# q and k of a dilated attention by seven products of quarters

## The chip, the cores and the metric

The kernel runs on one core of a Trainium2 chip. The metric is the device time of one execution in microseconds (us).

## What is computed

Two layers on a sequence of 512 tokens with 1024 features, all float32. Layer 0 has a gated recurrence (HGRN2), layer 1 a dilated attention; each is followed by a SwiGLU feed-forward part. The input of every part is normalised and modulated by vectors made from a condition `c`:

```python
mod = (cond @ ada_w[layer] + ada_b[layer])[:, None, :]
sh1, sc1, g1, sh2, sc2, g2 = jnp.split(mod, 6, axis=-1)
u = rms_norm(h, norm_g[layer, 0]) * (1.0 + sc1) + sh1
y = hgrn2_mixer(...) if layer % 2 == 0 else dilated_attention_mixer(u, cos, sin, w_in, w_out)
h = h + (1.0 + g1) * rms_norm(y, norm_g[layer, 1])
```

The attention has three groups (dilations 1, 4, 16), and in each group q, k and v for 8 heads of 128 features:

```python
proj = (u @ w_in).astype(jnp.float32).reshape(B, S, N_GROUPS, 3, ATT_HEADS, ATT_HEAD_DIM)
for gi, (window, dilation) in enumerate(DILATED_GROUPS):
    q = apply_partial_rope(proj[:, :, gi, 0], cos, sin) * scale     # turns the first 32 features
    k = apply_partial_rope(proj[:, :, gi, 1], cos, sin)
    o_g, lse_g = dilated_group_attention(q, k, proj[:, :, gi, 2], window, dilation)
```

The three groups' outputs are mixed by a softmax over their `lse`.

## The kernel before

Every float32 product is made of three reduced-precision ones (`three`): both operands are split into `hi` (a cast to fp32r, on ScalarE) and `lo` (what is left, on VectorE), and the products hi hi, hi lo and lo hi are added up in one PSUM bank.

Weights come through one queue. `Stream` holds a list of items in the order of their use, loads them by SyncE (SP) into tiles named `raw` (two places of 1 MB; a new tile gets the place that comes free first), and hands out `hi` and `lo` tiles (three places of each). An item is a weight matrix ("w"), a chunk of `ada_w` for the modulation vectors ("ada": four VectorE steps over one raw tile, and after every second chunk an all-reduce over the partitions on GpSimd, POOL in the profile), a pair of rows, a small piece of work ("do"), or "quarters": a weight pair that is cut in four. `weave` sets the ada chunks between the weights: `weave(ws, others, first, every)` puts one group behind each `every`-th weight, from `first` on.

Attention first makes v of the first four heads for three groups (six items, one of them in the stage before), then loops over heads and groups. A turn of this loop takes one weight item with q's and k's columns, makes two `block`s of 24 matmuls of 512 columns into two PSUM banks, evacuates them (`qk_evac`) and turns the first 32 features of both (`turn_pair`, 64 partitions). In between, `fl.tick()` issues work of earlier heads: `scores` (products of q and k, mask, maximum, exponential, and sums that go through DRAM by GpSimd's DMAs, `scr`, `oR`, `oN`), the merge of the groups, transposes (`flip`), products with v. After head 4 stand the v of the last four heads.

The order on each engine in this loop is set by a scheduler at build time; the engines' queues run in order.

The feed-forward parts compute gate and up with seven products instead of eight (`seven_products`): the four quarters of the weights and of the tokens (by feature half and token half) are summed in seven pairs, each product is 128x512 by 512x256, and the results are sums of the seven. The token sums are made once (`token_sums`), the weights' sums for each block: one on GpSimd, two on VectorE (`sum_a`, `sum_b`, `sum_c`), and sums and three of the quarters are split in `hi` and `lo`. Line 791 casts the sums, 795 takes their rest; 767 and 771 do that for the three quarters.

## Time and profile before

| | |
|---|---|
| median of 3 runs | 1515.43 us (1515.34 to 1515.98) |
| profiled execution | 1515.4 us, of which 1513.7 are the span of the trace |
| TensorE busy | 1497.8 us |
| VectorE busy | 1032.8 us |
| ScalarE busy | 692.5 us |
| GpSimd busy | 245.0 us |
| TensorE clock granted | 0.997 |

Busy times are sums over the instructions of an engine; matmuls overlap, so that a busy TensorE isn't one at its peak. Line numbers in the profile are those of the code above. In its rows PE is TensorE's matmuls, PEld its weight loads, DVE VectorE, ACT ScalarE, POOL GpSimd and SP SyncE.

### The profile page before, as it was taken

The page shows a single profiled execution, that of the slowest core. Times are in us where ns is not written, and L with a number is a line of the kernel's source. Part 1 is how long each engine was busy: PE and PEld are TensorE (multiplying, and loading weights), DVE is VectorE, ACT ScalarE, POOL GpSimd, SP SyncE. Part 2 cuts the span into 40 slices and gives each one's busy share as a digit, 9 for nine tenths or more (in the row PEclk, how much of TensorE's full clock was granted, in tenths as well). Part 3 has the DMA queues.
Part 4 walks back from the last instruction along what each step waited for, and adds up shares of the span by engine and source line. Part 5 has one row for each costly group of instructions (what it writes and reads, how often), then busy time and mean ns, then how long its engine had stood idle before and what let it go on. Part 6 is the DMA issues. An engine that isn't in the chain of part 4 may idle for free.

```text
span 1513.7 us, 23113 instructions
## 1 busy us (share of the span) xinstructions
PE 1497.8 (99%) x9111; PEld 1324.4 (87%) x9111; DVE 1032.8 (68%) x1764; ACT 692.5 (46%) x1107; POOL 245.0 (16%) x212
## 2 busy tenths in 40 slices
PE   8999999999999999999999999999999999999998
PEld 6777888899999988889888888988888999999886
DVE  4587867588888896562567686345656978888633
ACT  4443443364444432372456665245645635544231
POOL 1011210051222211140010111000002212221100
PEclk9999999999999999999999999999999999999999
DMA  9654444324333356414644433533212333334521
GB/s 308 185 164 142 153 138 167 112 70 126 112 112 112 116 198 224 138 57 137 167 126 126 125 109 102 153 98 91 78 30 83 100 97 111 107 107 153 205 99 56
DMA packets 207645, 192.83 MB, mean 127 GB/s; under 512 B 6776, under 2 KB 166704, under 8 KB 207536
## 3 DMA queue, kind: packets, MB, share of 16 engines
q1 hardware_dynamic: 206000, 190.87, 41.0%
q8 instruction: 71, 1.16, 0.3%
q0 software_dynamic: 1024, 0.13, 0.2%
q10 hardware_dynamic: 512, 0.35, 0.1%
q14 instruction: 38, 0.31, 0.1%
HBM read 189.17 MB, written 2.16 MB: 126 GB/s over the span
## 4 chain that ended last, share of the span: by engine, by line
PE 93%; issue 2%; ACT 1%; DVE 1%; POOL 1%; DMA 1%; POOLq 0%; DVEq 0%; ACTq 0%
PE ps_mm L417 20%; PE ps_mm L419 20%; PE ps_mm L418 20%; PE ps_b L417 3%; PE ps_b L419 3%; PE ps_b L418 3%; PE ps_a L417 3%; PE ps_a L419 3%; PE ps_a L418 3%; PE ps_mm L1165 1%; PE ps_a L1165 1%; PE ps_a L1610 1%; PE ps_a L1592 1%; PE ps_mm L223 1%; PE ps_a L1659 1%
## 5 line engine op out<-in xcount | busy, mean ns | idle before, releaser
L417 PE MATMUL ps_mm<-uh,hi 128*128 128x512 f32 (+1 forms) x784 | 289.9, 370 | 0.0
L419 PE MATMUL ps_mm<-uh,lo 128*128 128x512 f32 (+1 forms) x784 | 288.6, 368 | 0.0
L418 PE MATMUL ps_mm<-ul,hi 128*128 128x512 f32 (+1 forms) x784 | 287.4, 367 | 0.0
L85 DVE TENSOR_TENSOR lo<-raw,hi 128x2048 fp32r<-128x2048 f32 x74 | 174.7, 2361 | 161.2 <-ACT hi L84 161.0
L84 ACT CAST hi<-raw 128x2048 fp32r<-128x2048 f32 x74 | 141.3, 1909 | 152.4 <-DMA raw<-in_ffn_w_out_dram 49.2
L417 PEld LDWEIGHTS ps_mm<-uh,hi 128*128 128x128 f32 x784 | 147.4, 188 | 31.6 <-issue 8.4
L419 PEld LDWEIGHTS ps_mm<-uh,lo 128*128 128x128 f32 x784 | 147.6, 188 | 23.4
L418 PEld LDWEIGHTS ps_mm<-ul,hi 128*128 128x128 f32 x784 | 147.5, 188 | 22.6
L791 ACT CAST hiq<-raw 128x1024 fp32r<-128x1024 f32 x72 | 72.4, 1052 | 72.4 <-DVE raw L779 71.0
L417 PE MATMUL ps_mm<-hi,oh 128*128 128x512 f32 x240 | 94.1, 392 | 0.0
L418 PE MATMUL ps_mm<-lo,oh 128*128 128x512 f32 x240 | 93.5, 390 | 0.0
L245 DVE SCALAR_TENSOR_TENSOR shared<-raw,cond,shared 128x512 f32<-128x512 f32 x98 | 73.4, 749 | 24.2 <-DMA raw<-in_ada_w_dram 22.5
L795 DVE TENSOR_TENSOR loq<-raw,hiq 128x1024 fp32r<-128x1024 f32 x72 | 84.9, 1219 | 0.0
L247 POOL PARTITION_ALL_REDUCE shared<-shared x12 | 39.9, 3323 | 239.8 <-DVE shared L245 239.8
L419 PE MATMUL ps_mm<-hi,ul 128*128 128x512 f32 x192 | 75.9, 395 | 0.0
L418 PE MATMUL ps_mm<-lo,uh 128*128 128x512 f32 x192 | 75.9, 395 | 0.0
L775 POOL TENSOR_TENSOR raw<-raw 128x512 f32<-128x512 f32 x36 | 57.9, 1608 | 105.4 <-DVE loq L771 45.7
L417 PE MATMUL ps_mm<-hi,uh 128*128 128x512 f32 x192 | 74.5, 396 | 0.0
L779 DVE TENSOR_TENSOR raw<-raw 128x1024 f32<-128x1024 f32 x36 | 44.1, 1225 | 40.9 <-POOL raw L775 40.9
L419 PE MATMUL ps_mm<-hi,ol 128*128 128x512 f32 x176 | 68.5, 389 | 0.0
L825 POOL TENSOR_TENSOR shared<-shared 128x256 f32<-128x256 f32 x36 | 30.2, 840 | 205.8 <-DVE shared L824 205.8
L417 PE MATMUL ps_a<-hi,oh 128*128 128x512 f32 x152 | 59.6, 392 | 0.0
(403 smaller groups left out, 3937.6 us busy)
## 6 DMA issues: line engine op xcount, KB each, us to landing
raw<-in_ada_w_dram SPq DMA_DIRECT2D x40, 1024.0 KB, 5.1
raw<-in_ffn_w_in_dram SPq DMA_DIRECT2D x144, 256.0 KB, 4.1
raw<-in_attn_w_in_dram SPq DMA_DIRECT2D x48, 512.0 KB, 5.1
raw<-in_ffn_w_out_dram SPq DMA_DIRECT2D x22, 1024.0 KB, 4.9
raw<-in_hgrn_w_in_dram SPq DMA_DIRECT2D x12, 1024.0 KB, 5.3
raw<-in_attn_w_in_dram SPq DMA_DIRECT2D x12, 1024.0 KB, 5.1
raw<-in_ffn_w_in_dram SPq DMA_DIRECT2D x8, 1024.0 KB, 5.1
first<-in_ada_w_dram SPq DMA_DIRECT2D x14, 512.0 KB, 7.6
```

Of the source, the lines that this page charges most:

```text
L84: self.nc.scalar.copy(hi, t)
L85: self.nc.vector.tensor_sub(lo, t, hi.bitcast(F32))
L245: dve.scalar_tensor_tensor(a, r[:, k], sc, a, op0=OP.mult, op1=OP.add)
L247: pool.partition_all_reduce(a, a, P, bass.bass_isa.ReduceOp.add)
L417: pe.matmul(ps, ah, bh, start=start, stop=False)
L418: pe.matmul(ps, ah, bl, start=False, stop=False)
L419: pe.matmul(ps, al, bh, start=False, stop=stop)
L775: pool.tensor_add(r[:, 2], r[:, 2], r[:, 0])
L779: dve.tensor_tensor(r[:, 0:2], r[:, 0:3:2], r[:, 1:2].broadcast_to((P, 2, 512)), op=OP.add)
L791: act.copy(hi, src)
L795: dve.tensor_sub(lo, src, hi.bitcast(F32))
L1165: pe.matmul(vbanks[hf, t], a, w, start=e == 0 and which == 0, stop=e == KT - 1 and which == 2)
```

## The change

The loop's two blocks become seven products of quarters as in the feed-forward part, 84 matmuls of 256 columns, into four PSUM banks. A weight item is of kind "quarters" (`aqk`), four loads of 256 KB. `Weights` splits three quarters (lines 1595, 1596), makes three sums on GpSimd (1600, 1604, 1608; 128x512, 128x1024, 128x512) and splits these (1615, 1616); the next pair's weights are prepared while a pair is computed. k and q are put together from the banks by VectorE and ScalarE, and a sum over both halves of k by GpSimd (1664).

The token sums need two tiles of 2 MB. One takes the place of the residual `h` (class `Held`): `h` is stored to DRAM (`kept`, four GpSimd DMAs at the end of the stage before) and loaded again after the loop. The turn now uses 128 partitions with 256 columns (four 32-row copies each way on ScalarE, shuffle and three steps on VectorE); the tables of cosines and sines are laid out for that. The scale of the scores moves into the step with the mask (q and k change sign with it, so the masks do too). `scores` come one tick later. The ada chunks stand behind every item from the third on, not behind every second from the seventh, and their order is (1,4), (1,3), (1,2) instead of (1,2), (1,4), (1,3).

```diff
+ADA_AT = (2, 1)
...
         def aqk(g, hd):
-            return ("w", tuple(AW[:, (g * 3 + k) * D + hd * P:(g * 3 + k) * D + (hd + 1) * P].rearrange(
+            return ("quarters", tuple(AW[:, (g * 3 + k) * D + hd * P:(g * 3 + k) * D + (hd + 1) * P].rearrange(
                 "(k p) n -> p k n", p=P) for k in range(2)))
...
-        items += weave(at, ada_seq((1, 2), (1, 4), (1, 3)), 6, 2)
+        items += weave(at, ada_seq((1, 4), (1, 3), (1, 2)), ADA_AT[0], ADA_AT[1])
...
+                    for t in range(NT):
+                        pool.dma_start(kept[t * P:(t + 1) * P, :], h[:, t])
...
+            def __init__(self):
+                self.raw = st.quarters()
+                self.R = st.part_tiles()
+                act.copy(self.R[0][:, 0:1536], self.raw[:, 512:])
+                dve.tensor_sub(self.R[1][:, 0:1536], self.raw[:, 512:], self.R[0][:, 0:1536].bitcast(F32))
+
+            def sum_a(self):
+                r = Q4(self.raw)
+                pool.tensor_add(r[:, 2], r[:, 2], r[:, 0])
+
+            def sum_b(self):
+                r = Q4(self.raw)
+                pool.tensor_tensor(r[:, 0:2], r[:, 0:3:2], r[:, 1:2].broadcast_to((P, 2, 512)), op=OP.add)
+
+            def sum_c(self):
+                r = Q4(self.raw)
+                pool.tensor_add(r[:, 3], r[:, 3], r[:, 1])
+
+            def parts(self, k):
+                if k == 0:
+                    self.S = st.part_tiles()
+                src = Q4(self.raw)[:, 1:3] if k == 0 else Q4(self.raw)[:, 0:4:3]
+                hi, lo = (Q4(t)[:, 2 * k:2 * k + 2] for t in self.S)
+                act.copy(hi, src)
+                dve.tensor_sub(lo, src, hi.bitcast(F32))
+                if k == 1:
+                    st.fill()
...
+        def qk_pair(hd, g, w, following, ticks):
...
+            run(half(0, 1), w.R, 0, u_of(0, 0))
+            run(half(0, 0), w.R, 512, t_of(2))
+            nxt = following()
+            act.copy(at(slice(1, 3), 0), both(b[0]))
+            run(half(1, 0), w.R, 1024, u_of(1, 0))
+            if nxt:
+                nxt.sum_a()
+                nxt.sum_b()
+            run(half(1, 1), w.S, 0, t_of(3))
+            dve.tensor_tensor(at(slice(0, 3, 2), 0), wide(at(2, 0)), both(b[1]), op=OP.add)
+            if nxt:
+                nxt.parts(0)
+                nxt.sum_c()
+            ticks()
+            run(half(2, 1), w.S, 1024, t_of(1))
+            run(half(2, 0), w.S, 512, t_of(0))
+            dve.tensor_tensor(at(slice(0, 3, 2), 1), wide(at(2, 0)), both(b[2]), op=OP.add)
+            act.copy(at(1, 1), of(half(2, 0)))
+            if nxt:
+                nxt.parts(1)
+            run(half(3, 0), w.S, 1536, u_of(1, 1))
+            dve.tensor_tensor(at(0, 1), at(0, 1), of(half(3, 0)), op=OP.add)
+            pool.tensor_tensor(at(1, every), at(1, every), wide(at(2, 1)), op=OP.add)
+            turn = t[:, 2 * S:2 * S + 256]
+            rot = t[:, 2 * S + 256:3 * S]
...
+            for j in range(4):
+                act.copy(as_of(turn[32 * j:32 * j + 32]), at(j // 2, j % 2)[0:32])
+            dve.stream_shuffle(rot, turn, [(i + 16) % 32 for i in range(32)])
+            dve.tensor_mul(rot, rot, angle[:, 1])
+            dve.tensor_mul(turn, turn, angle[:, 0])
+            dve.tensor_add(turn, turn, rot)
+            for j in range(4):
+                act.copy(at(j // 2, j % 2)[0:32], as_of(turn[32 * j:32 * j + 32]))
+            heads[hd]["k", g], heads[hd]["q", g] = t[:, 0:S], t[:, S:2 * S]
...
+        smx.close()
+        h.again()
+        for t in range(NT):
+            pool.dma_start(h[:, t], kept[t * P:(t + 1) * P, :])
```

What this makes of the queues shows at three places. SP's loads at the start of the loop, before (the number behind `raw` counts the items; 126 and 130 are ada chunks, 127, 128 and from 131 on the pairs):

```order
L66 DMA raw125_8557<-in_attn_w_in_dram 128x4x512
L66 DMA raw126_8563<-in_ada_w_dram 128x4x512
L64 DMA raw127_8673<-in_attn_w_in_dram 128x8x128 x2
L64 DMA raw128_8680<-in_attn_w_in_dram 128x8x128 x2
L66 DMA raw130_8687<-in_ada_w_dram 128x4x512
L64 DMA raw131_8797<-in_attn_w_in_dram 128x8x128 x2
L64 DMA raw132_8814<-in_attn_w_in_dram 128x8x128 x2
```

And now, from the first pair (96) on:

```order
L69 DMA raw95_6622<-in_ada_w_dram 128x4x512
L60 DMA raw96_6628<-in_attn_w_in_dram 128x4x128 x4
L69 DMA raw97_6648<-in_ada_w_dram 128x4x512
L60 DMA raw98_6767<-in_attn_w_in_dram 128x4x128 x4
L69 DMA raw100_6805<-in_ada_w_dram 128x4x512
L60 DMA raw101_6872<-in_attn_w_in_dram 128x4x128 x4
L69 DMA raw102_6947<-in_ada_w_dram 128x4x512
L60 DMA raw103_7014<-in_attn_w_in_dram 128x4x128 x4
```

A pair has four loads for two, and through its first eight pairs each is followed by a chunk of 1 MB.

GpSimd's queue early in the loop, before (ISA without operands is a change of its code library, ISA on `shared` an all-reduce, the DMAs those of the softmax sums):

```order
L247 ISA
L247 ISA shared_90<-shared_90 128x512
L1604 DMA scr_3051<-sN669_6802 128x4x2
L1616 DMA oR691_6991<-scr_3051 128x8
L247 ISA shared_90<-shared_90 128x512
L1622 DMA scr_3051<-sR681_6893 128x8
L1624 DMA oN692_7000<-scr_3051 128x4x2
```

Now, around the weights of the fourth and fifth pair (103 and 106):

```order
L1712 DMA scr_3052<-sN682_7046 128x4x2
L1600 TENSOR_TENSOR raw103_7014<-raw103_7014 128x512
L1724 DMA oR706_7358<-scr_3052 128x8
L1664 TENSOR_TENSOR qk690_7068<-qk690_7068 128x2x4x64
L1604 TENSOR_TENSOR raw103_7014<-raw103_7014 128x1024
L266 ISA
L266 ISA shared_90<-shared_90 128x512
L1608 ISA
L1608 TENSOR_TENSOR raw103_7014<-raw103_7014 128x512
L1600 TENSOR_TENSOR raw106_7164<-raw106_7164 128x512
L1604 TENSOR_TENSOR raw106_7164<-raw106_7164 128x1024
L1608 TENSOR_TENSOR raw106_7164<-raw106_7164 128x512
```

Where the queue held DMAs and all-reduces alone, every weight set now has three sums there and every pair one more; the library changes before an all-reduce and back after it.

VectorE's queue at the same place, now: the last two steps of chunk 105, the turn of the third pair (`qk690`), and behind it the rest of the fourth pair's sums (`loq11`):

```order
L264 SCALAR_TENSOR_TENSOR shared_90<-raw105_7097,cond_89,shared_90 128x512 x2
L1671 STREAM_SHUFFLE qk690_7068<-qk690_7068 128x256
L1672 TENSOR_TENSOR qk690_7068<-qk690_7068,shared_90 128x256
L1673 TENSOR_TENSOR qk690_7068<-qk690_7068,shared_90 128x256
L1674 TENSOR_TENSOR qk690_7068<-qk690_7068 128x256
L1616 TENSOR_TENSOR loq11_7132<-raw103_7014,hiq11_7131 128x1024
```

Before, the loop's weights and its turns stood like this there:

```order
L85 TENSOR_TENSOR lo133_9025<-raw133_8821,hi133_9024 128x2048
L1565 STREAM_SHUFFLE rot935_9017<-turning926_8958 64x512
L1566 TENSOR_TENSOR rot935_9017<-rot935_9017,shared_90 64x512
L1567 TENSOR_TENSOR turning926_8958<-turning926_8958,shared_90 64x512
L1568 TENSOR_TENSOR turning926_8958<-turning926_8958,rot935_9017 64x512
L85 TENSOR_TENSOR lo134_9109<-raw134_8929,hi134_9108 128x2048
```

One rest of 2048 columns a pair became one of 1536 and two of 1024, and the turn's steps are half as long.

More of the change, by code (lines that the diff above doesn't have):

```diff
@@ L109, in quarters @@
     def quarters(self):
+        while self.items[self.done][0] in ("ada", "rows", "do"):
+            self.process_to(self.done + 1)
         assert self.items[self.done][0] == "quarters"
@@ L198, in block_kernel @@
         shared = base.tile([P, 4, S], F32, name="shared")
-        cs = shared[:, 0:2]
+        cs, csr = (shared[:, k].rearrange("p (a n) -> p a n", a=2) for k in range(2))
         cols = base.tile([P, 8, 8], F32, name="cols")
@@ L1335, in tok_proj @@
                     w = slice((kt % 4) * 512, (kt % 4 + 1) * 512)
-                    three(ps, view(uh[:, kt])[t], view(ul[:, kt])[t], whi[:, w], wlo[:, w], kt == 0, kt == KT - 1)
+                    three(ps, *(view(x[kt // 4][:, kt % 4])[t] for x in fu), whi[:, w], wlo[:, w], kt == 0, kt == KT - 1)
                 act.copy(dst[:, t, c0:c0 + 512], ps)
@@ L1562, in turn_pair @@
-        def turn_pair(g, pair):
-            both = pair[0]
-            rot = fresh(mk, [64, S], "rot", 1)
-            dve.stream_shuffle(rot, both, [(i + 16) % 32 for i in range(32)])
-            dve.tensor_mul(rot, rot, cs[0:64, 1])
-            dve.tensor_mul(both, both, cs[0:64, 0])
-            dve.tensor_add(both, both, rot)
-            for k in range(2):
-                dst, src = pair[1 + k][0:32], both[k * 32:k * 32 + 32]
-                act.copy(*((dst, src) if g == 0 else (V4(dst), L4(src))))
+        smx = cx.enter_context(ExitStack())
@@ new lines, in block_kernel @@
+        sums_t = smx.enter_context(tc.tile_pool(name="a_sums", bufs=1)).tile(
+            [P, TPAD + 4096], F32R, name="sums_a")[:, TPAD:]
+        K4 = lambda t: t.rearrange("p (k n) -> p k n", k=4)
+        th_t = fresh(base, [P, NT, D], "h", 1, F32R)
+        th = [K4(th_t[:, k]) for k in range(4)]
+        tl = [K4(sums_t[:, k * 1024:(k + 1) * 1024]) for k in range(4)]
+        u_of = lambda r, c: [tuple(x[r][:, k, c * 256:c * 256 + 256] for x in fu) for k in range(4)]
+        t_of = lambda i: [(th[i][:, k], tl[i][:, k]) for k in range(4)]
@@ new lines, in qk_pair, with run @@
+        def qk_pair(hd, g, w, following, ticks):
+            b = [bank("mm") for _ in range(4)]
+            half = lambda n, k: b[n][:, k * 256:k * 256 + 256]
+            def run(ps, wt, o, us):
+                for kt in range(4):
+                    a = slice(o + kt * P, o + (kt + 1) * P)
+                    three(ps, wt[0][:, a], wt[1][:, a], *us[kt], kt == 0, kt == 3)
+            t = fresh(mk, [P, 3 * S], "qk", 2)
+            if g == 0:
+                at = lambda b_, h_: t.rearrange("p (b h n) -> p b h n", b=3, h=2)[:, b_, h_]
+                of = lambda a: a
+                both = lambda a: H2(a)
+            else:
+                at = lambda b_, h_: t.rearrange("p (b r h l) -> p b h r l", b=3, r=4, h=2)[:, b_, h_]
+                of = lambda a: a.rearrange("p (l r) -> p r l", r=4)
+                both = lambda a: a.rearrange("p (h l r) -> p h r l", h=2, r=4)
+            every = slice(0, 2)
+            wide = lambda a: a.unsqueeze(1).broadcast_to((P, 2) + tuple(a.shape[1:]))
+            run(half(0, 1), w.R, 0, u_of(0, 0))
[23 more added lines that the diff above has]
+            rot = t[:, 2 * S + 256:3 * S]
+            as_of = (lambda a: a) if g == 0 else (lambda a: a.rearrange("p (r l) -> p r l", r=4))
+            angle = cs if g == 0 else csr
+            for j in range(4):
[4 more added lines that the diff above has]
+            dve.tensor_add(turn, turn, rot)
+            for j in range(4):
+                act.copy(at(j // 2, j % 2)[0:32], as_of(turn[32 * j:32 * j + 32]))
+            heads[hd]["k", g], heads[hd]["q", g] = t[:, 0:S], t[:, S:2 * S]
+            ticks()
+            return nxt
@@ L1699, in block_kernel, with following @@
         fl.n = 0
-        for kind, g, i in order[1:]:
+        first_t, last_t = fresh(mk, [P, 3 * S], "qk", 2), fresh(mk, [P, 3 * S], "qk", 2)
+        for j in range(2):
+            token_sums(*([x[:, 2 * j:2 * j + 2] for x in y] for y in (th, tl)),
+                       [H2(first_t[:, k * S:k * S + S]) for k in range(3)] + [H2(last_t[:, j * S:j * S + S])],
+                       slice(2 * j, 2 * j + 2))
+        steps = order[1:]
+        ahead = []
+        def following():
+            w = Weights()
+            ahead.append(w)
+            return w
+        for n_, (kind, g, i) in enumerate(steps):
+            nxt = steps[n_ + 1][0] if n_ + 1 < len(steps) else None
             if kind == "v":
                 tok_proj(V[g], 0, nat if g == 0 else res, (0, 1, 2) if i and g == 0 else ())
+                if nxt == "qk":
+                    w = following()
+                    w.sum_a()
+                    w.sum_b()
+                    w.parts(0)
+                    w.sum_c()
+                    w.parts(1)
                 continue
@@ L1714, in block_kernel @@
                 fl.add(n + 11, lambda i=i: pv_n(i))
-            whi, wlo = st.take()
-            pair = []
-            for k in range(2):
-                ps = block(whi, wlo, k * D, P)
-                heads[i]["qk"[k], g] = qk_evac(ps, g, k, pair)
-                if k == 1:
-                    turn_pair(g, pair)
-                fl.tick()
+            qk_pair(i, g, ahead.pop(0), following if nxt == "qk" else lambda: None, fl.tick)
+        smx.close()
+        h.again()
+        for t in range(NT):
+            pool.dma_start(h[:, t], kept[t * P:(t + 1) * P, :])
         fl.at.clear()
```

64 lines of the change are left out of this document (36 added, 28 removed).

## The prediction

> **What bounds the kernel now.** I read the page first, then the stretches of attention, then single engines there. TensorE works nearly all the time, and the chain that ends last runs through it:
>
> ```profile
> PE 1497.8 (99%) x9111; PEld 1324.4 (87%) x9111; DVE 1032.8 (68%) x1764; ACT 692.5 (46%) x1107; POOL 245.0 (16%) x212
> ...
> PE 93%; issue 2%; ACT 1%; DVE 1%; POOL 1%; DMA 1%; POOLq 0%; DVEq 0%; ACTq 0%
> ```
>
> The stretch table has attention's v part (672 to 728), its whole q/k loop (728 to 1112) and a piece of the loop without modulation work (1040 to 1100):
>
> ```profile
> 672.00:728.00 56.00, 56.00 (x241) 54.08 (x241) 19.22 (x16) 17.03 (x16) 2.14 (x3) 1.00 0.43 125
> 728.00:1112.00 384.00, 384.00 (x1906) 333.30 (x1905) 235.06 (x624) 202.99 (x341) 39.81 (x36) 1.00 0.41 117
> 1040.00:1100.00 60.00, 60.00 (x303) 51.07 (x302) 39.41 (x125) 34.38 (x62) 3.95 (x6) 1.00 0.25 72
> ```
>
> TensorE is full in all three, at clock 1.00; VectorE has 66% in the last, GpSimd almost nothing. So less TensorE work is worth its time, until another engine is slower than what is left. That is the question here, since the change buys TensorE time with VectorE, ScalarE and above all GpSimd time.
>
> The loop's pace, from two matmuls 48 apart, the 48 evacuations of q and k, and the 12 of the three v blocks that interrupt the loop:
>
> ```profile
> 734.67 0.39 PE L418 MATMUL ps_mm<-ul,hi 128*128 128x512 f32 x1
> 745.55 0.39 PE L418 MATMUL ps_mm<-ul,hi 128*128 128x512 f32 x1
> L1557 ACT ACTIVATE qk<-ps_mm x48: 580/594/601, 728.6 to 1107.5; 128x512 f32<-128x512 f32 x48
> L1337 ACT COPY V<-ps_mm x12: 567/587/591, 928.8 to 990.2; 128x512 f32<-128x512 f32 x12
> ```
>
> A pair (q and k of one head in one group) has 48 matmuls: 745.55 - 734.67 = 10.88 us. Eleven steps of v take 61.4, so twelve 67.0. From 728.6 to 1107.5 are 47 half pairs and the v part: (378.9 - 67.0) / 23.5 = 13.27, say 13.2 us for a pair with its share of scores, transposes and weighted sums; those take TensorE 13.2 - 10.88 = 2.3.
>
> **The products.** The new pair has 84 matmuls of 256 columns. The feed-forward part runs the same seven products now; two successive blocks there, by the same step on VectorE:
>
> ```profile
> 454.80 2.35 DVE L795 TENSOR_TENSOR loq<-raw,hiq 128x1024 fp32r<-128x1024 f32 x2
> 464.46 2.36 DVE L795 TENSOR_TENSOR loq<-raw,hiq 128x1024 fp32r<-128x1024 f32 x2
> ```
>
> 9.66 us a block. TensorE's own gain is 10.88 - 9.66 = 1.22 a pair, 29.3 for 24 pairs, and its floor for a pair is 9.66 + 2.3 = 11.95.
>
> **What the helpers pay for a pair.** Groups of the page and of the instruction view (mean ns last but one):
>
> ```profile
> L85 DVE TENSOR_TENSOR lo<-raw,hi 128x2048 fp32r<-128x2048 f32 x74 | 174.7, 2361 | 161.2 <-ACT hi L84 161.0
> L771 DVE TENSOR_TENSOR loq<-raw,hiq 128x1536 fp32r<-128x1536 f32 x18 | 31.6, 1753 | 0.3 <-ACT hiq L767 0.2
> L795 DVE TENSOR_TENSOR loq<-raw,hiq 128x1024 fp32r<-128x1024 f32 x72 | 84.9, 1219 | 0.0
> L1565 DVE STREAM_SHUFFLE rot<-turning 64x512 f32<-64x512 f32 x24 | 17.4, 724 | 0.0
> L1566 DVE TENSOR_TENSOR rot<-rot,shared 64x512 f32<-64x512 f32 x24 | 16.3, 680 | 0.2
> L820 DVE TENSOR_TENSOR shared<-shared,ps_mm 128x512 f32<-128x512 f32 x18 | 12.3, 681 | 4.9 <-PE ps_mm L419 4.9
> L84 ACT CAST hi<-raw 128x2048 fp32r<-128x2048 f32 x74 | 141.3, 1909 | 152.4 <-DMA raw<-in_ffn_w_out_dram 49.2 <-PE ps_mm L418 42.3 <-DMA raw<-in_hgrn_w_in_dram 27.4
> L767 ACT CAST hiq<-raw 128x1536 fp32r<-128x1536 f32 x18 | 26.7, 1482 | 0.0
> L791 ACT CAST hiq<-raw 128x1024 fp32r<-128x1024 f32 x72 | 72.4, 1052 | 72.4 <-DVE raw L779 71.0 <-DVE raw L783 1.3
> L854 ACT COPY shared<-ps_a 128x256 f32<-128x256 f32 x18 | 6.7, 374 | 29.7 <-DVE mid L835 28.1 <-PE ps_b L419 1.6
> ```
>
> VectorE loses the rest of the weights (2.36), the shuffle (0.72) and three turning steps (3 x 0.68): 5.1. It gets the rest of three quarters (1.75), of four sums (2 x 1.22), two sums out of PSUM (2 x 0.68), one of half that (0.35), and the turn on 128 partitions with half the columns (0.36 + 3 x 0.36): 7.4. Net +2.3, on 39.41 / 60 x 13.2 = 8.7 before: 11.0. ScalarE swaps a 1.91 cast for 1.48 + 2 x 1.05, and its copies change little (eight of 32x256, each at most the 0.37 of 128x256): +2 on 34.38 / 60 x 13.2 = 7.6, so under 10: it stays behind TensorE and costs nothing. GpSimd gets everything new: three weight sums and k's sum. Its prices:
>
> ```profile
> L518 POOL TENSOR_TENSOR ul<-u,uh x20: 1277/1301/2538, 306.2 to 1180.4; 128x512 fp32r<-128x512 f32 x20
> L1384 POOL TENSOR_TENSOR k<-T,fsuf x8: 1048/1248/3198, 92.8 to 231.7; 128x512 f32<-128x512 f32 x8
> L247 POOL PARTITION_ALL_REDUCE shared<-shared x12 | 39.9, 3323 | 239.8 <-DVE shared L245 239.8
> 332.77 7.00 POOL L253 PARTITION_ALL_REDUCE shared<-shared  x2 [5.77 <-issue]
> 1.47 0.29 POOL masks.py:199 TENSOR_SCALAR_AFFINE_SELECT ident<-ident 128x128 f32<-128x128 f32 x1 [0.30 <-POOL expo L190]
> POOL oR L1616 <- DMA scr<-sN: 24.9, 8, 3.4
> ```
>
> Undisturbed, a 128x512 sum takes 1.28, so 128x1024 2.56, and one with a broadcast operand 1.05: 1.28 + 2.56 + 1.28 + 1.05 = 6.2 a pair.
>
> **The port.** Three rows of another stage decide the sum. A GpSimd sum and VectorE's L85 start together, then a small VectorE product follows:
>
> ```profile
> 167.97 3.20 POOL L1384 TENSOR_TENSOR k<-T,fsuf 128x512 f32<-128x512 f32 x1 [20.94 <-DVE T L1362]
> 167.97 2.29 DVE L85 TENSOR_TENSOR lo<-raw,hi 128x2048 fp32r<-128x2048 f32 x1
> 170.18 1.27 DVE L1385 TENSOR_TENSOR m<-T,f 128x256 f32<-128x256 f32 x1
> ```
>
> 3.20 is L85's time and then the sum's own 1.05; the 256-column product, worth 0.36, lasts until the GpSimd sum is over. They run one after the other, never together. So I add them. Of VectorE's pair the steps with both inputs in SBUF count: 1.75 + 2.44 + 3 x 0.36 = 5.3. With GpSimd's 6.2 that is 11.5, and about 0.4 of small steps of the softmax weights: 11.9, as much as TensorE's 11.95.
>
> The Trainium skill ("SBUF — State Buffer", section "Who interferes with whom") states this as a rule: a VectorE instruction with two SBUF inputs contends with a GpSimd instruction that reads SBUF, and the later one is blocked to the end. By that rule the addition holds for every pair; if the two shared bandwidth instead, the loop would go by TensorE's floor and VectorE's own 11.0 and 14.5, the first rival below. The three rows above agree with the page.
>
> **The eight pairs with modulation work.** Twelve chunks move from every second to every item, from the second v half on; four fall to the v part, eight to the first eight pairs. A chunk on VectorE, its columns, and the loads:
>
> ```profile
> 707.11 0.49 DVE L243 TENSOR_SCALAR shared<-raw,cond 128x512 f32<-128x512 f32 x1 [1.88 <-DMA raw<-in_ada_w_dram]
> 707.64 2.33 DVE L245 SCALAR_TENSOR_TENSOR shared<-raw,cond,shared 128x512 f32<-128x512 f32 x3
> L262 DVE CUSTOM_DVE_ANT_0 diag<-shared,ident 128x128 f32<-128x128 f32 x32 | 9.1, 286 | 4.1 <-POOL shared L247 3.8
> raw<-in_ada_w_dram SPq DMA_DIRECT2D x40, 1024.0 KB, 5.1
> raw<-in_ffn_w_in_dram SPq DMA_DIRECT2D x144, 256.0 KB, 4.1
> L57 SPq DMA_DIRECT2D raw<-in_ffn_w_in_dram x144: 367/501/788, 347.4 to 1360.2; - x144
> 333.33 3.27 DVE L106 TENSOR_TENSOR lo<-raw,hi 128x1024 fp32r<-128x1024 f32 x1
> ```
>
> VectorE: 11.0 + 2.9 + 4 x 0.29 / 2 = 14.5 a pair. An all-reduce holds the port too: the last row is one that ran beside the first all-reduce (from 332.77). Port: 11.5 + 2.3 + 0.6 + half an all-reduce 1.65 = 16.0. GpSimd by itself for two pairs: 12.4, one all-reduce 3.3, the 5.8 with which it waited for nothing visible before the first one at 332.77, the way back to sums, and for the softmax DMAs two thirds of about 7.5 (issues, and waits like the 24.9 / 8 = 3.1 of oR). No row shows the way back unhidden: 0.3 (the other switch that a row shows, at the start) to 5.8. I take 5.8, since that row is the same kind of switch in mid-kernel: 32 for two, 16 for one. The raw places: a quarter set is held from its load (the third piece issued 2 x 0.5 after the first, 5.1), through cast 1.5, rest 1.75, three sums 5.1, cast 1.05, to the last rest 1.2, 16 in all; a chunk 5.1 + 2.9. Two places, one of each per pair: 12. So port and GpSimd set these pairs at 16.0, with no loss between them; I take 16.5, between that and 18.5, which is a queue of 16 with 15% lost.
>
> The Trainium skill ("GPSIMD Engine Reference", section "Instruction dispatch") puts a load of about 6 us on the first call of a freshly loaded GpSimd kernel. By that both ways cost 6 and the sum stays as it is; by the 0.3 row GpSimd has 13.5 a pair, and the port alone decides. The 5.77 agrees with the page for the one way; no run here shows the other.
>
> **The other parts.** The sixteen later pairs: TensorE 11.95 and port 11.9 cannot both be full, since each waits at times for the other; I take 13.0, from 11.95 (no loss) to 14.2 (a sixth lost). The token sums are 24 VectorE steps of 128x512 (L820's 0.68 each, 16 us), and with three chunks they stand beside the casts of the v part, where VectorE had 19.22 of 56: hidden; +2 for the first pair's chain behind two all-reduces, from 0 (ready before v ends) to 5 (one switch and one sum late). The four stores of the residual stand on GpSimd's queue ahead of the masks only; what waits for them is the casts of the token sums, which have the whole v part; without that cover a store's 5 us. The reload is issued when the loop ends and needed at the first update:
>
> ```profile
> 1150.12 1.42 DVE L480 SCALAR_TENSOR_TENSOR h<-yg,rr,h 128x512 f32<-128x512 f32 x2 [0.27 <-POOL rr L470]
> ```
>
> That is 38 us after 1112, for 2 MB: 0, and without cover some 10. On SP's queue a pair has four issues for two, 1.0 us more of a queue that is idle most of a pair. Masks, angles at half width and the scores a tick later: 0, beside a full TensorE; the turn's chain after a pair (0.35 + 1.05 + 8 x 0.37 + 1.4, 6 us) is shorter than the pair that hides it, and costs its excess if GpSimd is late.
>
> **Sum**, against the profiled execution (1515.4, span 1513.7; the median of the runs is 1515.43): eight pairs 8 x (16.5 - 13.2) = +26; sixteen 16 x (13.0 - 13.2) = -3; start +2. Together +25: 1540. TensorE's 29.3 is in these numbers, and is eaten by waiting.
>
> **Rivals.**
> *The port does not bind.* GpSimd's reads fall into VectorE's gaps (PSUM sums, waits), so eight pairs go by VectorE's 14.5 and sixteen by TensorE's 11.95: +10 - 20 = -10, 1506; it decides for faster as soon as the eight stay under 15.7 with the sixteen at 11.95. For it: half of VectorE's time is PSUM or one-input work. Against it: 11.9 of 11.95. With nothing bound at all 24 x (11.95 - 13.2) = -30, 1485; the 14.5 speak against that.
> *Everything queues.* GpSimd is in order, so its waits for the softmax DMAs and the two switches stand ahead of the next pair's sums, and a late sum holds the raw place: 19 and 14.2, +46 + 16 + 3 = +65, 1580. For it: one switch pair stands between two sums of one weight set. Against it: a weight set is started a whole pair ahead.
> *No change*: the two effects cancel, 1512 to 1518.
>
> **Chances.** Forecast (1520 to 1562) 0.55; everything queues 0.17; faster 0.21; no change 0.07. A difference under 0.2% (3 us) can't be told from none. So slower 0.72, and the range from 1503 to 1580 leaves out one in ten at either end.
>
> **What would show it.** Right: TensorE idle by 50 us or more, nearly all between 725 and 870; GpSimd busy above 420 us; its 128x512 sums near 2 us on average and VectorE's 128x1024 rests above 1.22; pairs of 16 to 17 us first, near 13 later. Wrong: TensorE full in the first pairs, or sums at 1.3 with VectorE at its old durations.

## The result: 7.5% slower, and the profile after

The changed kernel takes 1629.31 us (median of 4 runs, 1628.01 to 1630.89) against 1515.7 for the kernel before: ratio 1.0747, interval 1.0728 to 1.0765. The forecast was 1540 with a range to 1580, so the sign was right and the size far off. Of the page after, its busy line and the two rows of the forty slices that changed most:

```profile
PE 1511.0 (93%) x9975; PEld 1370.2 (84%) x9975; DVE 1167.0 (72%) x1913; ACT 734.1 (45%) x1259; POOL 424.1 (26%) x316
...
PE   8999999999999999997577688998888999999998
...
PEclk9999999999999999998798899999998999999999
```

TensorE, 99% busy before, now has gaps from slice 19 on, which is the q/k loop, and in five of these slices its granted clock is below full. The second did not happen before, and the prediction has no word on it.

Once in each pair ScalarE copies a product (L1659), so its rows time the pairs; the first, the ninth, the last ahead of the v blocks, and the first and last behind them:

```profile
742.64 0.37 ACT L1659 COPY qk<-ps_mm 128x256 f32<-128x256 f32 x1 [2.57 <-DVE qk L1658]
...
917.21 0.37 ACT L1659 COPY qk<-ps_mm 128x256 f32<-128x256 f32 x1 [2.41 <-DVE qk L1658]
...
1011.72 0.35 ACT L1659 COPY qk<-ps_mm 128x256 f32<-128x256 f32 x1
1090.73 0.37 ACT L1659 COPY qk<-ps_mm 128x256 f32<-128x256 f32 x1
...
1211.58 0.36 ACT L1659 COPY qk<-ps_mm 128x256 f32<-128x256 f32 x1
```

Eight steps from the first to the ninth copy give 21.8 us a pair, six more 15.8, and eight behind the v blocks 15.1. Before, a pair took 13.2. The three stretches as windows (columns as in the prediction: span, PE, PEld, VectorE, ScalarE, GpSimd, clock, DMA share, GB/s):

```profile
733.00:917.00 184.00, 127.25 (x903) 121.58 (x902) 130.05 (x267) 79.38 (x160) 81.30 (x49) 0.84 0.32 93
917.00:1012.00 95.00, 79.07 (x597) 74.46 (x596) 78.43 (x167) 58.28 (x119) 43.68 (x27) 0.96 0.35 106
1079.00:1212.00 133.00, 116.86 (x955) 115.19 (x953) 107.88 (x216) 81.18 (x164) 62.26 (x43) 0.96 0.25 72
```

In the first, the slowest of the three, no engine is full: VectorE has 71%, TensorE 69%, GpSimd 44%. GpSimd's figure leaves out its changes between all-reduce and sums, four pairs of them in this stretch (rows under e1): with these 55 us its queue is held for 136 of 184 us, 74%, and its waits for the softmax DMAs come on top. Still every engine has room, so the time is at least in part one of waiting in turn and not of one engine's load alone. What TensorE waits for between 725 and 1230 us, the three largest:

```profile
PE ps_mm L436 <- ACT hiq L1615: 30.2, 10, 9.7
PE ps_a L1718 <- ACT qk L1676: 20.2, 5, 10.3
PE ps_mm L438 <- DVE loq L1616: 10.9, 8, 3.5
```

The first and the third are the split sums of a weight set (the tiles prepared for one pair), the second is the turned q and k that the scores need (total us, times, longest).

**TensorE's account.** From 600 us on (nothing differs ahead of that) I added up the distances between the starts of successive matmuls. Where a row shows a wait, the wait is taken out; in stretches at granted clock 0.5, half the distance is put down to the clock; the rest is work. The same for the experiments below:

| kernel | us, median | waits | half clock | work |
|---|---|---|---|---|
| before | 1515.7 | 3 | 0 | 903 |
| after | 1629.3 | 102 | 32 | 886 |
| e17, the change with plain products | 1553.5 | 24 | 8 | 912 |
| e2, all sums on VectorE | 1575.8 | 55 | 24 | 887 |
| e1, partition sums on TensorE | 1602.5 | 69 | 37 | 890 |
| e18, large sum on VectorE | 1617.6 | 86 | 35 | 887 |
| e4, e1 and e18 together | 1571.8 | 51 | 19 | 890 |
| o7, e4 and chunks as pieces | 1558.8 | 47 | 13 | 889 |
| e13, o7 without any sums | 1530.4 | 29 | 8 | 886 |
| e14, o7 with plain products | 1548.0 | 17 | 5 | 917 |

After less before is 99 us of waits and 32 of half clock, less 17 of work: 114, the measured 113.6. So TensorE got 17 us, and waits and half clock took back more than seven times as much.

### The profile page after: what moved, and what is told of

Read it like the earlier page. It is cut to its first block, busy times and chain, and to the rows that moved or that the text cites. A ratio compares the mean times of both kernels' runs of the same rounds, so it can differ in the third digit from the quotient of the medians.

```text
span 1626.3 us, 25598 instructions
## 1 busy us (share of the span) xinstructions
PE 1511.0 (93%) x9975; PEld 1370.2 (84%) x9975; DVE 1167.0 (72%) x1913; ACT 734.1 (45%) x1259; POOL 424.1 (26%) x316
## 5 line engine op out<-in xcount | busy, mean ns | idle before, releaser
L436 PE MATMUL ps_mm<-h,hiq 128*128 128x256 f32 x384 | 114.8, 299 | 30.2 <-ACT hiq L1615 30.2
L436 PE MATMUL ps_mm<-uh,hi 128*128 128x512 f32 (+1 forms) x400 | 139.1, 348 | 0.0
L438 PE MATMUL ps_mm<-uh,lo 128*128 128x512 f32 (+1 forms) x400 | 137.2, 343 | 0.0
L437 PE MATMUL ps_mm<-ul,hi 128*128 128x512 f32 (+1 forms) x400 | 136.8, 342 | 0.0
L438 PE MATMUL ps_mm<-h,loq 128*128 128x256 f32 x384 | 113.2, 296 | 11.0 <-DVE loq L1616 10.9
L437 PE MATMUL ps_mm<-sums_a,hiq 128*128 128x256 f32 x384 | 112.7, 294 | 0.0
L438 PE MATMUL ps_mm<-uh,loq 128*128 128x256 f32 x360 | 103.6, 288 | 5.2 <-DVE loq L1596 5.2
L436 PE MATMUL ps_mm<-uh,hiq 128*128 128x256 f32 x360 | 104.6, 292 | 2.9 <-ACT hiq L1595 2.0
L436 PEld LDWEIGHTS ps_mm<-h,hiq 128*128 128x128 f32 x384 | 78.3, 204 | 32.3 <-ACT hiq L1615 32.3
L437 PE MATMUL ps_mm<-ul,hiq 128*128 128x256 f32 x360 | 103.2, 288 | 0.0
L264 DVE SCALAR_TENSOR_TENSOR shared<-raw,cond,shared 128x512 f32<-128x512 f32 x98 | 79.7, 814 | 13.8 <-DMA raw<-in_ada_w_dram 12.7
```

Source lines behind the costliest of these rows:

```text
L264: dve.scalar_tensor_tensor(a, r[:, k], sc, a, op0=OP.mult, op1=OP.add)
L436: pe.matmul(ps, ah, bh, start=start, stop=False)
L437: pe.matmul(ps, ah, bl, start=False, stop=False)
L438: pe.matmul(ps, al, bh, start=False, stop=stop)
```

## The experiments

Theory S: GpSimd's changes between the all-reduce and the sums hold its queue. Theory Q: the sums themselves, on GpSimd's queue and on its port with VectorE. Theory C, later R: the crowded chunks, or the raw places that they hold. From e9 on, theory V: VectorE's time is what binds; theory L: the latency of a pair's chain. The medians of before were 1515.7 to 1517.1 in all sets.

**e1: partition sums on TensorE**

```
-                if kq == 1 and (l, v) != (0, 5):
+                if kq == 1 and (l, v) != (0, 5) and not sum_pe(l, v):    # v in (2, 3, 4)
```

> The changed kernel, with the six partition sums of the modulation that fall into attention made by TensorE with a matrix of ones (as layer 0's modulation is already) instead of GpSimd's all-reduce, so that GpSimd has only the sums of weights and of k there and never changes its kernel. Theory S (switches): the way back costs GpSimd as much as the way there, 7.1 us each by the trace after, so an all-reduce blocks the queue of sums for 17.4 us, TensorE starves behind it, and its clock halves after each such wait; the first eight pairs then fall from 20.3 to 14 to 15 us and the later ones, without the backlog, to about 14: 1629 - 45 - 35 = about 1550. Theory Q (queues and port): the load of VectorE and GpSimd on one port and the in-order queue of sums are the cause, the switches only a part: no more than 40 us come back, 1590 or more.

Measured 1602.5, ratio 1.0563 (1.0546 to 1.0581): 27 us back. By S's own figure (1550) S falls as the main cause, though its price is real; Q had 1590 or more. Three of the all-reduces in the kernel after, each with the next GpSimd sum behind it:

```profile
751.52 3.25 POOL L266 PARTITION_ALL_REDUCE shared<-shared  x1 [7.13 <-issue]
761.86 1.25 POOL L1600 TENSOR_TENSOR raw<-raw 128x512 f32<-128x512 f32 x1 [7.10 <-issue]
...
789.71 3.25 POOL L266 PARTITION_ALL_REDUCE shared<-shared  x1 [5.89 <-DMA raw<-in_attn_w_in_dram]
799.78 1.25 POOL L1608 TENSOR_TENSOR raw<-raw 128x512 f32<-128x512 f32 x1 [6.82 <-issue]
...
880.93 3.25 POOL L266 PARTITION_ALL_REDUCE shared<-shared  x1 [6.04 <-DVE shared L264]
891.02 1.25 POOL L1664 TENSOR_TENSOR qk<-qk 128x512 f32<-128x512 f32 x1 [6.85 <-issue]
```

GpSimd stands still for 5.9 to 7.1 us ahead of these all-reduces and for 6.8 to 7.1 us behind them: one takes 16 to 17.5 us of its queue. (The third may also have waited for VectorE's L264, which its row names; the first names nothing.) The prediction's 5.8 for the unknown way back was low by 1.0 to 1.3. The Trainium skill ("GPSIMD Engine Reference", section "Instruction dispatch") has about 6 us for the first call of a freshly loaded kernel; the trace's waits, in both directions, are near that figure or up to a fifth above it.

**e2: all sums on VectorE**

```
-                pool.tensor_add(r[:, 2], r[:, 2], r[:, 0])
+                dve.tensor_add(r[:, 2], r[:, 2], r[:, 0])      # sum_a; so too sum_b, sum_c, k's sum
```

> The changed kernel with the three sums of weights and the sum of k on VectorE instead of GpSimd; the all-reduces stay on GpSimd, which then has one kernel only. No switch and nothing on the shared port, but VectorE gets 0.68 + 1.22 + 0.68 + 0.68 = 3.3 us a pair more: 11.0 + 3.3 = 14.3, with modulation work 17.8. Theory S: without the switches VectorE is what binds, 24 x 14.3 + 8 x 3.5 = 371 against 317 for the loop before, about 1560. Theory Q: the port and the queue of sums cost more than VectorE's 3.3 us a pair, so this is the fastest of the four, 1530 to 1550, and faster than the run with TensorE's partition sums.

Measured 1575.8, ratio 1.0391 (1.0376 to 1.0407): 53 us better than after, but slower than both forecasts (about 1560 and 1530 to 1550). The loop's windows, first of after, then of e2, with e2's parts ahead of and behind the v blocks:

```profile
733.00:1212.00 479.00, 390.17 (x2756) 375.15 (x2754) 336.06 (x703) 240.45 (x479) 196.15 (x127) 0.92 0.29 84
```

```profile
733.00:1164.00 431.00, 387.65 (x2771) 371.16 (x2770) 340.04 (x804) 241.80 (x481) 35.32 (x37) 0.95 0.34 100
733.00:982.00 249.00, 207.88 (x1514) 196.02 (x1513) 210.62 (x491) 139.28 (x282) 25.35 (x21) 0.91 0.37 108
1048.00:1164.00 116.00, 113.77 (x962) 112.21 (x962) 107.46 (x257) 81.82 (x167) 8.12 (x13) 1.00 0.37 110
L1604 DVE TENSOR_TENSOR raw<-raw 128x1024 f32<-128x1024 f32 x24 | 29.2, 1218 | 0.1
L1600 DVE TENSOR_TENSOR raw<-raw 128x512 f32<-128x512 f32 x24 | 16.4, 683 | 0.1
```

This is the clearest reading of the port. On VectorE the four sums take 29.2 + 3 x 16.4 = 78 us. Yet VectorE is busy 340 us with them and 336 without them: GpSimd's sums, which VectorE does not execute, make its other instructions longer by nearly what they would cost it themselves. Behind the v blocks e2 has hardly a loss left: TensorE is 98% busy there at clock 1.00. What e2 still loses in the loop stands ahead of them. Two consecutive steps of the turn in the kernel after, under GpSimd's sums, show how:

```profile
924.39 1.29 POOL L1600 TENSOR_TENSOR raw<-raw 128x512 f32<-128x512 f32 x1 [4.93 <-DMA raw<-in_attn_w_in_dram]
925.76 2.46 POOL L1604 TENSOR_TENSOR raw<-raw 128x1024 f32<-128x1024 f32 x1
```

```profile
924.71 1.25 DVE L1672 TENSOR_TENSOR qk<-qk,shared 128x256 f32<-128x256 f32 x1
925.88 2.61 DVE L1673 TENSOR_TENSOR qk<-qk,shared 128x256 f32<-128x256 f32 x1
928.42 0.68 DVE L1658 TENSOR_TENSOR qk<-qk,ps_mm 128x512 f32<-128x512 f32 x1
...
L1658 DVE TENSOR_TENSOR qk<-qk,ps_mm x24: 653/680/690, 741.9 to 1208.2; 128x512 f32<-128x512 f32 x24
...
L1673 DVE TENSOR_TENSOR qk<-qk,shared x24: 409/420/2622, 747.7 to 1218.0; 128x256 f32<-128x256 f32 x24
```

Both VectorE steps end 0.3 us after the GpSimd sum beside them, whatever their own length: 1.25 and 2.61 for two steps worth 0.42. The last two rows give shortest, median and longest of 24: L1673, with both inputs in SBUF, ranges to 2622 ns; L1658, with one input in PSUM, never exceeds 690. Only two of the 24 L1658 ran beside a GpSimd sum, though; the one that did so from end to end, at 864.48, took 674.

**e3: chunks as far apart as before**

```
-ADA_AT = (2, 1)
+ADA_AT = (6, 2)
```

> The changed kernel with the modulation's twelve chunks at every second item from the seventh on (as before the change) instead of at every item from the third. Nothing else changes: the same six all-reduces, each with both switches, fall over twice as many pairs. Theory S: six times the same price, so the time stays within 15 us of 1629. Theory C (crowding): it is the crowding of the chunks into eight pairs (two raw places, VectorE at 14.5 us a pair) that starves TensorE: 1629 - 40 or more, 1590 or less.

Measured 1644.4, ratio 1.0833 (1.0813 to 1.0853), 15 us slower than after. C falls: spreading the chunks out does not help. That the same six all-reduces then disturb more pairs would fit the 15 us, but no run shows it.

**e4 and e18: the large sum on VectorE, with TensorE's partition sums (e4) and in the change alone (e18)**

```
-                pool.tensor_tensor(r[:, 0:2], r[:, 0:3:2], r[:, 1:2]...
+                dve.tensor_tensor(r[:, 0:2], r[:, 0:3:2], r[:, 1:2]...
```

> The changed kernel with the partition sums on TensorE as in the first run and besides the 128x1024 sum of weights on VectorE (as in the feed-forward part), so GpSimd has 6.2 - 2.4 = 3.8 us a pair left, VectorE 11.0 + 1.2 = 12.2, the two together 5.3 + 1.2 + 3.8 + 0.4 = 10.7 on the port instead of 11.9. Theory S: the first run has the switches out of the way already, so this one is within 8 us of it. Theory Q: port and queue are relieved by a tenth, and the chain of a weight set is 1.2 us shorter and free of GpSimd's largest piece: 15 us or more below the first run.

> The changed kernel with the 128x1024 sum of weights on VectorE and nothing else: GpSimd keeps the all-reduces, the switches, two 128x512 sums and the sum of k. Without the switches the same move brought 31 us (1602.5 to 1571.8). If the two causes only add up, this is 1629 - 31 = 1598; if the sums suffer more behind a switch, where they start late, the move brings more, 1590 or less.

Measured 1571.8, ratio 1.0363 (1.0346 to 1.0379), and 1617.6, ratio 1.0662 (1.0643 to 1.0682). With e1 this is a square. The move of the large sum brings 31 us without the switches (1602.5 to 1571.8) but 12 with them (1629.3 to 1617.6); taking the switches away brings 27 with the large sum on GpSimd and 46 with it on VectorE; both together 57.5. The two do not add up: while one is there, removing the other frees less. That both stand in the one queue that every weight set passes would explain it; the square itself shows only that they depend on each other. Both forecasts for e18 (1598, 1590) were wrong in that they took the causes as independent or the switch as making the sums worse. For e4 theory S had at most 8 us below e1 and falls again.

**o5 to o8 and e12: chunks as pieces in a place of their own**

```
-        items += weave(at, ada_seq((1, 4), (1, 3), (1, 2)), ADA_AT[0], ADA_AT[1])
+        items += at
...
+                t = piece.tile([P, 512], F32, ..., tag="piece", bufs=1)
+                nc.sync.dma_start(t, src)          # one piece of 128x512 at each tick
```

> The changed kernel, with the loop's modulation weights no longer in the two raw places: they come as 48 pieces of 128x512 (and four rows) through a 2-KB tile of their own, one at each tick of the loop. The six all-reduces stay on GpSimd with their switches. Theory R (raw places): in the trace of the changed kernel the loads of the weight sets of the first eight pairs start 743.3, 763.7, 785.2, 813.1, 832.3, 849.0, each when the last rest of the set before is taken, because the second place holds a chunk; so a pair lasts as long as one set holds its place, 20.3 us on average. With both places for sets two are in flight, and those pairs go at the 15 to 16 us of the later ones: 1629 - 8 x 4.5 = about 1593. Theory Q (queues and port): GpSimd's queue and the shared port hold a set back wherever it lies, so the place changes nothing: 1620 or more.

> As the run before it, and the partition sums on TensorE, so that GpSimd never changes its kernel: the sums of weights and k alone stay on it. Against the run with TensorE's partition sums and the chunks in raw places (1602.5): theory R says 8 x 4.5 = 36 less, about 1566; theory Q 1595 or more. If both causes are separate, this is about 27 below the run before it.

> As the run before it, and the 128x1024 sum of weights on VectorE. Against the same with the chunks in raw places (1571.8, first pairs at 18.5): theory R says the first pairs go at the 14.1 of its pairs behind v: 1571.8 - 8 x 4.4 = about 1537; theory Q 1560 or more, since VectorE, at 16 to 19.9 of each 20 us from 800 on there, gets no work less.

> The changed kernel with the chunks in a place of their own and all sums of weights and of k on VectorE; GpSimd has the all-reduces alone (no switch). Against the same with the chunks in raw places (1575.8): theory R says 30 to 36 less, about 1542; if VectorE's load is what binds (14.3 us a pair, 17.8 with modulation work, which is only spread differently now), the time stays at 1560 or more.

> The fastest so far (1558.8 us: chunks in their own place, partition sums on TensorE, the 128x1024 sum on VectorE), with the sum of k on VectorE too. GpSimd keeps two 128x512 sums of weights. VectorE gets 24 x 0.68 = 16 us of work and loses the stretch that 31 to 39 us of GpSimd's sums of k bring it, some 12 to 15. Theory V: about even, 1552 to 1564. If ScalarE's copies that wait for GpSimd's sum of k (the turn begins with them) are what holds the pair: 1550 or less.

Measured against their partners without pieces: o5 1652.5 (+23), o6 1599.0 (-3.5), o7 1558.8 (-13), o8 1576.4 (0 to 1); e12, with k's sum moved too, 1560.4, even with o7 as forecast. R's 36 us are nowhere. But the test is not clean: the pieces are issued on the same SP queue as the sets, and in o5 five of them, waiting for their one place, hold it for 25.67 us, so that the next set is loaded 31 us after the one before:

```profile
748.25 3.46 SPq L60 DMA_DIRECT2D raw<-in_attn_w_in_dram  x4
751.82 25.67 SPq L1588 DMA_DIRECT2D piece<-in_ada_w_dram  x5
779.39 2.03 SPq L60 DMA_DIRECT2D raw<-in_attn_w_in_dram  x4
```

What the raw places cost by themselves stays open; no run had a third one.

**e9, e10: one more addition a pair, on VectorE (with e2) or GpSimd (with e4); e11: e4 with the softmax's merges, transposes and weighted sums a tick later.** In e11 one head's last weighted sums come behind the second v block and read the later heads' v, so values differ, not the work.

```
+            dve.tensor_add(extra[:, 0:768], both_sc[:, 0:768], both_sc[:, 0:768])     # e9; e10: pool, 512 columns
...
-                fl.add(n + 8, lambda i=i: (merge_r(i), merge_n(i)))
+                fl.add(n + 8 + (i < 6), lambda i=i: (merge_r(i), merge_n(i)))          # e11; so the next four
```

> The kernel with all sums on VectorE (1575.8 us) and one more VectorE addition in each pair, 128x768 from SBUF to SBUF (some 0.95 us), into a tile that nobody reads. Theory V (VectorE's time): in that kernel VectorE is busy 340 of the loop's 431 us, and outside the three v blocks nearly always, so every microsecond more of it lengthens the loop: 24 x 0.95 = 23, about 1597. Theory L (latency: engines wait for one another along the chain of a pair, and each has room): the extra step falls into VectorE's gaps, 1582 or less.

> The kernel with the partition sums on TensorE and the 128x1024 sum on VectorE (1571.8 us), and one more GpSimd addition of 128x512 in each pair (1.28 us, 31 us in all), into a tile that nobody reads. GpSimd is busy 5 to 8 of every 20 us there, so for its own queue this is nothing. Theory P (port): GpSimd's sums stop VectorE while they overlap; in the changed kernel 157 us of them lengthened VectorE's instructions by 62, so 31 us cost VectorE some 12 and, VectorE being the bound, the kernel as much: 1580 to 1587. Without the port as a cause: within 3 us of 1571.8.

> The kernel with the partition sums on TensorE and the 128x1024 sum on VectorE (1571.8 us), with the merging of the softmax weights, the transposes of the probabilities and the weighted sums each a tick (half a pair) later for heads 0 to 5. The same work, with more time between a step and who needs it. Theory L: TensorE's waits for the scaled probabilities (6.4 us there, 18 to 23 in others) and what follows from them go: 1560 or less. Theory V: the work is the same, 1568 to 1576.

Measured 1591.4 (+15.6 on e2) and 1589.5 (+17.8 on e4), which look like answers and are none. Where the added rows ran:

```profile
L1658 DVE TENSOR_TENSOR extra<-shared x24: 941/948/955, 682.4 to 755.8; 128x768 f32<-128x768 f32 x24
```

```profile
L1659 POOL TENSOR_TENSOR extra<-shared x24: 1029/1368/3107, 679.5 to 736.6; 128x512 f32<-128x512 f32 x24
```

All 24 stand between 680 and 756 us, in the v part and at the loop's start: since they depend on nothing in the loop, the scheduler drew them ahead. They are no load in each pair, and both are void for their question; in e10 the loop's first copy comes 20 us later than in e4 and its last one 20, so it priced a late start. e11 took 1577.7, 6 us more than e4: more time for the softmax steps does not help, as theory V expected (1568 to 1576, missed by 2).

**e13 to e17: is TensorE's saving there, and what is the rest of the change worth?** e13 leaves out the sums of weights and of k (q and k have other values), e14 has plain products in all pairs of o7, e15 and e16 seven products in every second and third pair only, e17 the change as it is with plain products in all pairs.

```
+                if plain:
+                    act.copy(self.R[0], self.raw)
+                    dve.tensor_sub(self.R[1], self.raw, self.R[0].bitcast(F32))
+                    st.fill()
+                    return
```

> The fastest so far (1558.8 us: chunks in their own place, partition sums on TensorE, the 128x1024 sum on VectorE), leaving out the three sums of weights and the sum of k (so the values of q and k are not right; casts, rests and all 84 matmuls of a pair are kept). VectorE loses 24 x 1.22 = 29 us of work and the 44 us that GpSimd stretched it by, and a set of weights is ready 4 us earlier. Theory V (VectorE's time binds): the loop falls to TensorE's floor of 11.95 a pair, 1495 to 1510. If something else holds the pairs (order, places, latency of the casts): 1535 or more.

> The fastest so far with all 24 pairs by plain products (48 matmuls of 512 columns, a cast and a rest of 128x2048) in place of the seven; all else of the change stays: token sums, residual in DRAM, turn on 128 partitions, scores a tick later, with the chunks in their own place and the partition sums on TensorE. Theory V: the loss is the seven products' helpers, so this is within 10 us of the kernel before, 1512 to 1525. If the moved residual, the token sums or the later scores carry a part, it is 1530 or more.

> The fastest so far with seven products in every second pair and plain ones between. Theory V: VectorE has some 13 us in a pair of seven products and 8 in a plain one, 10.6 on average, under TensorE's (11.95 + 13.2) / 2 = 12.6, so TensorE binds again and gains 12 x 1.22 = 15 us on the run with plain products alone: about 1503. Theory L (each set of seven products comes late by its own chain): half the loss remains, 1535.

> As the run before it, with seven products in every third pair. Theory V: 8 x 1.22 = 10 us below the run with plain products alone, about 1508. Theory L: 1528.

> The changed kernel, all 24 pairs by plain products (48 matmuls of 512 columns, one cast and one rest of 128x2048, no sums of weights or of k); everything else as in the change: chunks in the raw places at every item from the third, all-reduces on GpSimd, which has no other kernel now, token sums, residual in DRAM, later scores, turn on 128 partitions. If the 32 us of the run with plain products belong to the change's other parts, this is 1540 or more, and the seven products with their helpers cost 1629 - 1545 = 85. If they belong to the pieces and TensorE's partition sums, it is 1515 to 1525, and the seven products cost 105 to 115.

Measured: e13 1530.4, ratio 1.0097 (1.0082 to 1.0112); e14 1548.0; e15 1541.1; e16 1542.8; e17 1553.5, ratio 1.0249 (1.0232 to 1.0266). Windows from 600 to the end, of before, of e17 and of e13:

```profile
600.00:1513.60 913.60, 903.59 (x5144) 807.71 (x5142) 581.39 (x1070) 430.86 (x682) 130.71 (x116) 1.00 0.37 111
```

```profile
600.00:1550.80 950.80, 919.96 (x5147) 813.70 (x5145) 569.90 (x1094) 441.77 (x786) 140.82 (x124) 0.99 0.37 112
```

```profile
600.00:1529.60 929.60, 894.34 (x6046) 836.33 (x6044) 637.96 (x1182) 472.63 (x834) 114.52 (x118) 0.99 0.37 114
```

Three things follow. First, the seven products cost 1629.3 - 1553.5 = 76 us in this change although they save TensorE 912 - 886 = 26. Second, 38 us have nothing to do with them: e17 has plain products and VectorE less busy than before, and still waits 24 us, loses 8 to the clock, and has 9 us more work. Some 5 of these come from its 512-column matmuls, which start a median of 233 ns apart (227 before; by the mean of unbroken runs 231 against 227). Of its waits 15 us lie in the first pairs (750 to 824 us), the longest at TensorE's scores, which wait for the turned q and k:

```profile
757.32 3.36 PE L1732 MATMUL ps_a<-qk 128*128 128x128 f32 x8 [7.50 <-ACT qk L1708]
```

Third, on one and the same base (o7) plain products take 1548.0, seven products without any sums 1530.4, with sums 1558.8: 18 us gained by the products, 28 lost by the sums. e15 is the mixture of both, and its 7 us on plain products are half of what theory V wanted. Theory V's times (e13 1495 to 1510, e14 1512 to 1525, e15 1503, e16 1508) were all too low, and theory L's for e15 and e16 (1535, 1528) too. No version beats the kernel before; of those that do the whole computation e15 is the fastest.

## Why the prediction was wrong, step by step

**Right.** The direction; the port (the fence under e2); the way back of the switch; GpSimd above 420 us (424.1); TensorE's saving in the products (29.3 forecast, 26 by e17 against after, 17 against before); TensorE's waits above 50 us. Not their place: of 102 us only 41 stand between 725 and 870, where "nearly all" was expected.

The 89 us between 1540 and 1629 by place: the eight pairs 42, the sixteen later ones 38, the rest of the kernel some 9. By cause they overlap: the 38 of "the other parts" and the 32 of the clock below lie for the most part inside the pairs.

**"The eight pairs with modulation work", 16.5.** They took 21.8, which is 8 x 5.3 = 42 us of the 89 missing. The step added up each resource's load (port 16.0, GpSimd 16, VectorE 14.5) and took the largest. The windows above show none of them full, and GpSimd at 74% with its changes. A weight set goes ScalarE, VectorE, GpSimd, ScalarE, VectorE in turn, each engine in order with other work between, and an all-reduce of 16 to 17.5 us in the middle holds up every step behind it. "With no loss between them" was the error; "everything queues" had the mechanism and put it at 19. By the same copies e1, without the switches, takes 19.2 us for each of these pairs, and e2, with neither the switches nor the sums on GpSimd, 18.4. So moving both off GpSimd takes away less than half of what these pairs have over 13.2; the rest stays in e2 though VectorE, which makes the sums there, is only 83% busy:

```profile
741.00:887.90 146.90, 118.25 (x807) 109.99 (x806) 122.43 (x280) 75.94 (x154) 20.62 (x14) 0.88 0.38 109
```

**"The raw places: 12".** That shared 16 us of a set and 8 of a chunk between two places, as if neither was ever held for longer. In the trace after, the loads of successive sets start at 743.30 and 763.70, 20.4 us apart, with one chunk's load between. Whether the places set the pace was not settled (o5 to o8).

**"The sixteen later pairs", 13.0.** 15.8 and 15.1: (2.8 x 6 + 2.1 x 10) = 38 us. These have no chunks behind 917 us, and still VectorE has 81 to 83% and TensorE waits. The copy of e1 and of e2 behind the v blocks (first and last start of nine) tells which helper it is:

```profile
L1660 ACT COPY qk<-ps_mm x9: 359/366/372, 1068.7 to 1189.2; 128x256 f32<-128x256 f32 x9
L1659 ACT COPY qk<-ps_mm x9: 349/369/374, 1057.5 to 1161.6; 128x256 f32<-128x256 f32 x9
```

Without the switches (e1) a pair takes 15.1 there, as in the change; with the sums on VectorE (e2) it takes 13.0, the prediction's figure. So in the late pairs the 2.1 us are the price of having the sums on GpSimd and not on VectorE.

**"Its 128x512 sums near 2 us".** They were 1.41 to 1.66 on average, because VectorE, not GpSimd, paid for most collisions: the three small steps of the turn, priced at 0.36 and 0.42 when undisturbed, took 0.66 to 1.12 on average. The price of the port was sought on the wrong engine:

```profile
L1604 POOL TENSOR_TENSOR raw<-raw 128x1024 f32<-128x1024 f32 x24 | 60.7, 2529 | 1.6
...
L1600 POOL TENSOR_TENSOR raw<-raw 128x512 f32<-128x512 f32 x24 | 34.9, 1453 | 119.8 <-DVE loq L1596 51.7 <-DMA raw<-in_attn_w_in_dram 33.0 <-issue 14.3
```

```profile
L1673 DVE TENSOR_TENSOR qk<-qk,shared 128x256 f32<-128x256 f32 x24 | 26.9, 1122 | 0.0
```

**"The other parts", +2.** By e17 they cost 38; in proportion no term was further off. Its 48 evacuations of q and k show that most of it lies inside the loop:

```profile
L1663 ACT ACTIVATE qk<-ps_mm x48: 581/589/607, 735.2 to 1141.2; 128x512 f32<-128x512 f32 x48
```

That is 406.0 us from first to last, against 378.9 before: 27 of the 38, and the first eight pairs make 23 of these (122.9 us against 100.3). Each edit was put at nothing under a cover of its own, a full TensorE or the v part, and none was bounded together with the rest. Which of them carries it (later scores, the turn's eight copies, moved residual, token sums, chunks behind every item) was not tried one by one.

**The clock.** No term for it: 32 us. Windows around one wait, and matmuls of that time:

```profile
757.70:764.50 6.80, 3.32 (x29) 3.12 (x28) 5.97 (x19) 0.37 (x1) 2.56 (x2) 1.00 0.00 0
764.51:771.33 6.82, 3.87 (x16) 3.57 (x16) 3.63 (x5) 4.60 (x8) 4.82 (x3) 0.50 0.55 155
771.34:778.10 6.76, 5.69 (x45) 5.15 (x45) 4.29 (x7) 5.84 (x15) 1.61 (x2) 1.00 0.52 156
```

```profile
767.00 0.58 PE L436 MATMUL ps_mm<-h,hiq 128*128 128x256 f32 x1 [5.97 <-ACT hiq L1615]
...
769.49 0.41 PE L437 MATMUL ps_mm<-sums_a,hiq 128*128 128x256 f32 x1
769.71 0.41 PE L438 MATMUL ps_mm<-h,loq 128*128 128x256 f32 x1
...
772.65 0.28 PE L436 MATMUL ps_mm<-h,hiq 128*128 128x256 f32 x1
772.76 0.28 PE L437 MATMUL ps_mm<-sums_a,hiq 128*128 128x256 f32 x1
```

After a wait of 5.97 us TensorE comes back at granted clock 0.50, and its matmuls start 0.22 us apart until 771.3, then 0.11. Of the 6.8 us at half clock TensorE works the last 4.3, so this wait costs about 2 us more. The Trainium skill ("TensorE: Matmul & The Clock Gate", section "Part 1: The HAM clock gate") says that an idle window of about 3.4 us halves the clock and that a busy one restores it; the trace agrees in the length: the half-clock stretches of this loop last 3.4, 6.8 and 10.2 us. The length of a wait alone does not decide it here: one of 2.94 us that ended at 871.55 was followed by such a stretch, one of 3.54 us that ended at 1117.83 was not. The prediction forecast 50 us of waits and did not ask how long a single one would be.

**What stays open.** How the waits ahead of the v blocks divide between VectorE's time (e2: 211 of 249 us there) and the latency of the chain: the two runs meant to tell this apart, e9 and e10, were void. e13 takes the sums' load and their step in the chain away at once and finds 28 us on o7.

## What to carry to other kernels

A load sum per engine is only a floor; where a datum passes four engines in order, look for the longest hold in its path and add the waits. Work given to GpSimd beside a busy VectorE is not taken off VectorE when both read SBUF (336 against 340 us here), so count it for both. And a TensorE that was never idle has a full clock to lose: in this kernel 102 us of waits brought 32 more at half clock.

## What the runs showed of the hardware that was not expected

- GpSimd's change between all-reduce and tensor sums took 5.9 to 7.1 us on the way there and 6.8 to 7.1 on the way back.
- 78 us of sums, moved from GpSimd to VectorE, left VectorE's busy time as it was (336 to 340 us).
- Plain matmuls of 512 columns started a median of 233 ns apart in e17, with u in halves, 227 before; no run tells why.
